# Down projection: gated tiles 3 to 18 as four block groups of four in one chain

## The chip, the cores and the metric

One core of one Trainium2 chip runs the whole program once. The metric is the device time of that launch in microseconds; the time before is the median of three runs.

## The reference, cut to what matters

Two layers of a sequence model, 1040 frames (16 meta tokens and 1024) by 1024 features, end each with a gated convolution block and a residual. The change lies in the last product of that block:

```python
def conv_ffn(x, w_up, conv_w, conv_b, w_down):
    h = x @ w_up
    ...
    u, g = jnp.split(hc, 2, axis=-1)
    return (jax.nn.silu(g) * u) @ w_down
...
h = h + conv_ffn(rms_norm(h, ffn_norm[i]), w_up[i], conv_w[i], conv_b[i], w_down[i])
```

silu(g) * u is 2816 wide, that is 22 tiles of 128 features, here called gated tiles; w_down turns them into 1024 output features, 8 output rows of 128.

## The kernel before

All data lie transposed: features on the 128 partitions, frames along the free axis, in two halves of 520 frames (layer 1, which drops the meta tokens at the end: 512). Every fp32 operand is split into a rounded part hi and a rest lo, and a product of two such operands is three matmuls (`mm3`, lines 256 to 258: hi x hi, lo x hi, hi x lo). A half of 520 frames is two pieces of 260 columns, a half of 512 one piece.

The up projection makes the gated tiles one by one and POOL's queue writes each to DRAM (`actd`). The residual stream lies in DRAM too (`hm`). The down projection (`ffn_down`, line 1648) then works through the tiles by a list, GROUPS. "n" is a plain group: for each of the 8 output rows and both halves it multiplies every tile, ACT copies the sum out of PSUM (line 1688), and an accumulating DMA of POOL's queue adds it to hm (line 1690). "r" is a plain group that adds on DVE straight to the residual, held in h tiles that were loaded from hm (`load_residual`, line 1658; line 1686). "s" is a block group (`down_blocks`, line 1557): the tiles, the output rows and the frames are each taken in two halves, and Strassen's scheme in Winograd's form computes the 2 x 2 x 2 block product with seven products instead of eight. The output rows go in four pairs j; a product is called (j, p) with p from 1 to 7. A group of eight tiles has four tiles to a product, a group of four has two.

For a product of a pair, `block_operand` (line 1109) makes the weight block: the raw blocks A11, A12, A21, A22 are loaded by SP, DVE combines them (line 1118: S1, S2, the difference for p = 7 in A21, S4), ACT casts hi (line 1136) and DVE subtracts to lo (line 1137). This is asked for AHEAD = 4 products early; hi and lo tiles alternate between two pools with three buffers each. After a product, `evacuate` (line 1593) empties PSUM: ACT copies after p = 1, 6, 7 and 4 (line 1596), DVE adds after p = 2, 5 or 7, and 3 (line 1595). Products 1, 6, 7 and 4 of a pair go on in the same bank, so PE may write p = 7 only after the copy of p = 6, and p = 4 only after that of p = 7; 5 and 3 share bank p2, which the add of p = 3 frees for the next pair's p = 5. A finished row is handed on (line 1584): accumulated into hm by POOL's queue (line 1590), or added on DVE to h (line 1587) where the residual is loaded already.

The block operands X1 to X7 of the moving side are made by a generator, `prepare` (line 1449): it loads four half-tile pairs by SP, forms four sums or differences on DVE (line 1519) and splits each of seven operands (ACT line 372, DVE line 373), eleven DVE rows and seven ACT casts of 1040 elements for four tiles. `pump` (line 1550) moves it on while slots (one-row SBUF buffers, 33 and 6) are free, and `complete` runs it until a group's operands are all there.

GROUPS before: tiles 0 to 2 plain, 3 to 10 a block group of eight, 11 to 14 plain onto the residual, 15 to 18 a block group of four; then `down_last` does 19 to 21. PE's order is the program's. The other engines' order is made by a scheduler, except for what `keep_in_program_order` pins.

## Time and profile before

| | us |
|---|---|
| median of 3 runs | 2485.22 (2484.97 to 2487.58) |
| the profiled execution | 2487.36 |
| its span | 2485.5 |
| PE busy | 2451.5 |
| DVE busy | 1879.0 |
| ACT busy | 1331.7 |
| down projection, layer 0: plain tiles begin, block group of four ends | 1006 and 1208 |
| down projection, layer 1: the same | 2240 and 2438 |

The span is the time between the program's first and last instruction; the profiled execution's own time is 1.9 us longer. Busy times are of one engine each, and the engines work side by side: only the one that the others wait for sets the time. A row of the timeline has the start, the duration, the engine, the line, the operation and the tiles (written<-read), and in brackets how long the engine stood idle before it and what ended that.

### The profile page before, as it was taken

To read this page: it belongs to the slowest core of one execution; us is meant where nothing else is said; L and a number is where in the kernel's file an instruction comes from. 1 tells how busy PE (TensorE), PEld (TensorE's weight loads), DVE (VectorE), ACT (ScalarE), POOL (GpSimd) and SP (SyncE) were. 2 spreads that over 40 slices of the span, in tenths; PEclk is the share of its full clock that TensorE was granted. 3 is DMA by queue.
4 is the path that set the end of the run, shared out by engine and by line. 5 is a ranking of instruction groups with operands and counts; after the bars stand their busy time and mean duration, and the time that the engine had idled before them with its cause. 6 is when DMAs were issued, how large, how long until landed. Compare 5 with 4: busy or idle time off the path is not lost.

```text
span 2485.5 us, 47396 instructions
## 1 busy us (share of the span) xinstructions
PE 2451.5 (99%) x18286; PEld 2358.8 (95%) x18286; DVE 1879.0 (76%) x3821; ACT 1331.7 (54%) x2889; POOL 388.3 (16%) x567
## 2 busy tenths in 40 slices
PE   9999999999999999999999999999999999999998
PEld 8989999999999999999999899999999999997887
DVE  7656776869988888865866666777799888887667
ACT  7346666636555555642543466665465555555433
POOL 2023333210000000100210334331100000001002
PEclk9999999999999999999999999999999999999999
DMA  4232134433322214764412222243423212247722
GB/s 134 69 88 70 45 97 128 127 124 102 119 76 80 90 66 143 196 165 126 129 43 70 75 79 72 67 147 106 147 84 110 90 64 90 83 159 168 213 72 87
DMA packets 122002, 261.02 MB, mean 105 GB/s; under 512 B 15264, under 2 KB 37024, under 8 KB 121776
## 3 DMA queue, kind: packets, MB, share of 16 engines
q1 hardware_dynamic: 97440, 182.81, 24.0%
q0 software_dynamic: 22464, 72.88, 10.4%
q8 instruction: 143, 2.34, 0.4%
q10 hardware_dynamic: 1872, 2.31, 0.3%
q14 instruction: 83, 0.68, 0.1%
HBM read 177.31 MB, written 67.85 MB: 99 GB/s over the span
## 4 chain that ended last, share of the span: by engine, by line
PE 70%; issue 15%; DVE 9%; ACT 4%; DMA 1%; POOL 1%; SPq 0%; DVEq 0%; POOLq 0%; ACTq 0%
PE mm L256 7%; PE mm L258 7%; PE mm L257 7%; PE up L257 6%; PE up L258 6%; PE up L256 6%; PE down L257 5%; PE down L256 5%; PE down L258 5%; PE av L755 3%; PE tr L729 2%; DVE S L696 1%; PE S L693 1%; PE wo L258 1%; PE wo L256 1%
## 5 line engine op out<-in xcount | busy, mean ns | idle before, releaser
L257 PE MATMUL up<-x,lo 128*128 128x260 f32 x2240 | 632.8, 283 | 1.1 <-DVE lo L1137 1.1
L256 PE MATMUL up<-x,hi 128*128 128x260 f32 x2240 | 632.9, 283 | 0.3 <-ACT hi L1136 0.3
L258 PE MATMUL up<-x,hi 128*128 128x260 f32 x2240 | 632.9, 283 | 0.0
L257 PEld LDWEIGHTS up<-x,lo 128*128 128x128 f32 x2240 | 421.7, 188 | 1.6 <-DVE lo L1137 1.5
L256 PEld LDWEIGHTS up<-x,hi 128*128 128x128 f32 x2240 | 421.6, 188 | 0.6 <-ACT hi L1136 0.5
L258 PEld LDWEIGHTS up<-x,hi 128*128 128x128 f32 x2240 | 421.9, 188 | 0.0
L1136 ACT CAST hi<-raw 128x512 fp32r<-128x512 f32 (+1 forms) x490 | 266.5, 553 | 210.8 <-PE up L258 91.3
L256 PE MATMUL mm<-xh,hi 128*128 128x348 f32 (+4 forms) x1056 | 362.9, 344 | 0.0
L1137 DVE TENSOR_TENSOR lo<-raw,hi 128x512 fp32r<-128x512 f32 (+1 forms) x490 | 287.6, 602 | 79.2 <-ACT hi L1136 78.7
L258 PE MATMUL mm<-xl,hi 128*128 128x348 f32 (+4 forms) x1056 | 339.9, 322 | 0.0
L257 PE MATMUL mm<-xh,lo 128*128 128x348 f32 (+4 forms) x1056 | 339.5, 321 | 0.0
L256 PEld LDWEIGHTS mm<-xh,hi 128*128 128x128 f32 x1056 | 199.5, 189 | 5.2 <-issue 4.6
L257 PEld LDWEIGHTS mm<-xh,lo 128*128 128x128 f32 x1056 | 199.5, 189 | 0.7 <-issue 0.7
L258 PEld LDWEIGHTS mm<-xl,hi 128*128 128x128 f32 x1056 | 198.4, 188 | 0.4 <-issue 0.3
L1118 DVE TENSOR_TENSOR raw<-raw,raw 128x512 f32<-128x512 f32 (+1 forms) x230 | 147.4, 650 | 32.0 <-DMA raw<-in_wd_dram 29.3
L708 ACT ACTIVATE P<-S,m 116x460 f32<-116x460 f32 (+2 forms) x224 | 125.0, 562 | 72.3 <-DVE m L696 68.6
L257 PE MATMUL down<-x,lo 128*128 128x260 f32 (+1 forms) x504 | 161.2, 320 | 0.4 <-DVE lo L1137 0.4
L256 PE MATMUL down<-x,hi 128*128 128x260 f32 (+1 forms) x504 | 161.1, 320 | 0.2 <-DVE dg L1595 0.2
L258 PE MATMUL down<-x,hi 128*128 128x260 f32 (+1 forms) x504 | 161.1, 320 | 0.0
L373 DVE TENSOR_TENSOR PT<-tr,PT 116x464 fp32r<-116x464 f32 (+3 forms) x240 | 123.0, 515 | 47.4 <-ACT PT L372 45.8
L223 ACT CAST hi<-raw 128x512 fp32r<-128x512 f32 (+2 forms) x152 | 87.3, 575 | 105.4 <-PE wo L258 34.0
L1397 POOL DMA_DIRECT2D actd<-cv x44 | 23.6, 537 | 737.4 <-DVE cv L1396 719.2
(308 smaller groups left out, 5985.6 us busy)
## 6 DMA issues: line engine op xcount, KB each, us to landing
raw<-in_wm_dram SPq DMA_DIRECT2D x330, 256.0 KB, 3.0
raw<-in_wd_dram SPq DMA_DIRECT2D x48, 256.0 KB, 4.6
actd<-cv POOLq DMA_DIRECT2D x22, 520.0 KB, 3.0
actd<-cv POOLq DMA_DIRECT2D x22, 512.0 KB, 3.2
cb<-cd SPq DMA_DIRECT2D x16, 520.0 KB, 4.0
hm<-h POOLq DMA_DIRECT2D x32, 260.0 KB, 3.1
kA<-kA SPq DMA_DIRECT2D x24, 260.0 KB, 4.1
kL<-kL SPq DMA_DIRECT2D x24, 260.0 KB, 4.7
```

Of the source, the lines that this page charges most:

```text
L223: nc.scalar.copy(hi[:, :n, :], raw[:, :n, :])
L256: nc.tensor.matmul(ps, wh, xh[:, c0:c0 + n], start=first, stop=False, skip_group_check=more)
L257: nc.tensor.matmul(ps, wl, xh[:, c0:c0 + n], start=False, stop=False, skip_group_check=more)
L258: nc.tensor.matmul(ps, wh, xl[:, c0:c0 + n], start=False, stop=last, skip_group_check=more)
L373: nc.vector.tensor_tensor(out=lo, in0=src, in1=hi.bitcast(F32), op=ALU.subtract)
L693: nc.tensor.matmul(S[:rows, :n], q["qA"][e][:, qs], q["kA"][e][:, c0:k1], start=True, stop=False)
L708: nc.scalar.activation(P[:rows, :n], S[:rows, :n], AF.Exp, scale=-1.0, bias=m[:rows, nch - 1:nch], accum_out=(den if nch == 1 else d3[:row ...
L729: nc.tensor.transpose(tr[:w, 3 - j, :rows], P[:rows, o:o + w], id_)
L755: nc.tensor.matmul(av[:, a:b], w.rearrange("p a b -> p (a b)"), x, start=(t == ts[0] and part == 0 and i == 0), stop=(t == last and i == 1))
L1118: nc.vector.tensor_tensor(out=q[out][:, :nk, :], in0=q[a][:, :nk, :], in1=q[b][:, :nk, :], op=op)
L1136: nc.scalar.copy(hi[:, :nk, :], src[:, :nk, :])
L1137: nc.vector.tensor_tensor(out=lo[:, :nk, :], in0=src[:, :nk, :], in1=hi[:, :nk, :].bitcast(F32), op=ALU.subtract)
```

## The change

Tiles 3 to 18 become four block groups of four, run as one chain of 16 row pairs: the sequence of products goes on across the group's borders, so the first product of a group stands among the last of the one before. The plain group "r" is gone. Rows of the first three groups, and the first pair of the fourth, are accumulated into hm by POOL's queue (24 and 2 of them, with LANDING = 8 products until a slot is free again); the residual's h rows are loaded in three portions at p = 6 of the fourth group's first three pairs, and its last three pairs are added to h on DVE. In a group of four, A11 and A12 come in one load into one tile, as do A21 and A22; S1 and S2 share a tile; the loads are asked for when the pair two before it reaches p = 6. Operands of the next group are pumped within the chain, two products out of three, and inside the chain the weight combines, weight splits and operand rows are pinned to program order (`placed`), while evacuations are not.

```diff
-GROUPS, LAST = (("n", 0, 3), ("s", 3, 8), ("r", 11, 4), ("s", 15, 4)), (19, 3)
+GROUPS, LAST = (("n", 0, 3), ("s", 3, 4), ("s", 7, 4), ("s", 11, 4), ("s", 15, 4)), (19, 3)
-LANDING = 4
+LANDING = 8
...
+            if nk == 2:
+                for names, src, own in ((("A11", "A12"), u, True), (("A21", "A22"), g, False)):
+                    t = self.wp.tile([128, 4, 128], F32, tag="raw", name="raw", bufs=4) if own else \
+                        fw.tile([128, 4, 128], F32, tag="raw2", name="raw2")
+                    nc.sync.dma_start(t[:], src)
...
+            self.placed(nc.vector.tensor_tensor(out=q[out][:, :nk, :], in0=q[a][:, :nk, :], in1=q[b][:, :nk, :], op=op))
...
+    def placed(self, ins):
+        if self.among_blocks:
+            self.tc.keep_in_program_order(ins)
...
+        self.placed(nc.scalar.copy(hi[:, :nk, :], src[:, :nk, :]))
+        self.placed(nc.vector.tensor_tensor(out=lo[:, :nk, :], in0=src[:, :nk, :], in1=hi[:, :nk, :].bitcast(F32),
+                                            op=ALU.subtract))
...
-            while len(ahead) < 2 and loads:
+            while len(ahead) < (1 if kind == "s" and self.among_blocks else 2) and loads:
...
+                    hi_ = nc.scalar.copy(h, src[:, :m, :W])
+                    lo_ = nc.vector.tensor_tensor(out=l, in0=src[:, :m, :W], in1=h.bitcast(F32), op=ALU.subtract)
+                    if self.among_blocks:
+                        self.tc.keep_in_program_order(hi_)
+                        self.tc.keep_in_program_order(lo_)
...
-                if nk == 2 and p == 6 and j + 1 < NP:
-                    self.block_raws(wd(2 * j + 2), wd(2 * j + 3), nk, j + 1, fw, raws)
+                if p == 6:
+                    for i in range(j + 1, min(j + 3, N)):
+                        self.block_raws(*wd(i), nk, i, fw, raws)
...
-            if hT:
+            m = 2 * (j % NP) + half
+            if j > N - NP:
...
+                if p == 1 and j % NP == 0:
+                    complete(lambda: built(groups[j // NP]))
...
+                if p == 6 and j >= N - NP and j < N - 1:
+                    load_residual({0: (2, 3), 1: (4, 5), 2: (6, 7, 0, 1)}[j - N + NP])
+                if i % 3 and (j >= N - NP or not built(groups[j // NP + 1])):
                     self.pump(1, 4)
```

`prepare` also got six more points at which it may pause among the blocks.

The first place is the beginning of layer 0's block groups on DVE, from the add onto dg of pair 0 to the first splits of pair 1. Line 1595 of before is 1628 of the change, 1118 is 1129, 1137 is 1152, 373 is 1532 and 1519 is 1539; raw2 names are S1, S2 or A21, st and t2 the operands' sums, du and dg the output rows. Before, in the group of eight:

```order
L1118 TENSOR_TENSOR raw2_14120<-raw2_13992,raw2_13994 128x512
L1118 TENSOR_TENSOR raw2_13992<-raw_13990,raw2_13992 128x512
L1137 TENSOR_TENSOR lo_13836<-raw_13630,hi_13835 128x512
L1137 TENSOR_TENSOR lo_13865<-raw_13642,hi_13864 128x512
L1118 TENSOR_TENSOR raw_13642<-raw_13642,raw2_13897 128x512
L1137 TENSOR_TENSOR lo_13900<-raw2_13897,hi_13899 128x512
L1118 TENSOR_TENSOR raw2_14122<-raw2_14120,raw_13990 128x512
L1595 TENSOR_TENSOR dg_13892<-down_13839,dg_13892 128x520
L1137 TENSOR_TENSOR lo_13930<-raw2_13895,hi_13929 128x512
L1595 TENSOR_TENSOR du_13772<-down_13903,du_13772 128x520
L1137 TENSOR_TENSOR lo_13961<-raw2_13638,hi_13960 128x512
```

Now, in the first group of four, with tiles 7 to 10's operands in it:

```order
L1628 TENSOR_TENSOR dg_13812<-down_13783,dg_13812 128x520
L1152 TENSOR_TENSOR lo_13780<-raw_13601,hi_13779 128x256
L1152 TENSOR_TENSOR lo_13797<-raw_13609,hi_13796 128x256
L1539 TENSOR_TENSOR st_13131<-st_13137,st_13131 128x1040
L1628 TENSOR_TENSOR du_13732<-down_13829,du_13732 128x520
L1539 TENSOR_TENSOR t2_13816<-st_13131,st_13128 128x1040
L1129 TENSOR_TENSOR raw2_13818<-raw2_13611 128x256
L1628 TENSOR_TENSOR du_13732<-down_13783,du_13732 128x520
L1129 TENSOR_TENSOR raw2_13818<-raw2_13818,raw_13609 128x256
L1539 TENSOR_TENSOR st_13128<-st_13137,t2_13816 128x1040
L1152 TENSOR_TENSOR lo_13822<-raw2_13818,hi_13821 128x256
L1532 TENSOR_TENSOR x6_13844<-t2_13816,x6_13843 128x1040
```

The split of (1,6), lo_13822, now follows two sums and a difference of the operands (st_13131, t2_13816, st_13128) and the two combines of its own pair; before, the combines stood early and no row of 1040 elements was there.

ACT at the same place, from the copy of (1,1) or the casts beside it. Before:

```order
L1596 COPY du_13803<-down_13778 128x520
L1136 CAST hi_13835<-raw_13630 128x512
L1596 COPY du_13772<-down_13747 128x520
L1136 CAST hi_13864<-raw_13642 128x512
L1136 CAST hi_13899<-raw2_13897 128x512
L1596 COPY dg_13892<-down_13747 128x520
L1136 CAST hi_13929<-raw2_13895 128x512
L1136 CAST hi_13960<-raw2_13638 128x512
L1596 COPY dg_13892<-down_13747 128x520
L1136 CAST hi_13998<-raw_13990 128x512
```

Now (line 1531 is the operand's cast, 1629 the copy out of PSUM, 1151 the weight's cast):

```order
L1629 COPY du_13751<-down_13738 128x520
L1531 CAST x1_13753<-st_13128 128x1040
L1151 CAST hi_13757<-raw2_13603 128x256
L1629 COPY du_13732<-down_13719 128x520
L1531 CAST x2_13774<-st_13134 128x1040
L1629 COPY dg_13812<-down_13719 128x520
L1151 CAST hi_13779<-raw_13601 128x256
L1151 CAST hi_13796<-raw_13609 128x256
L1629 COPY dg_13812<-down_13719 128x520
L1151 CAST hi_13821<-raw2_13818 128x256
L1531 CAST x6_13843<-t2_13816 128x1040
```

The casts x1, x2 and x6 of 1040 elements now stand between the copies of pair 0 and 1.

The second place is on DVE late in the chain. Before, in layer 0's group of four, from the combine S2 of pair 2 (raw2_15429), whose split lo_15432 stands three rows below the last of these:

```order
L1118 TENSOR_TENSOR raw2_15429<-raw2_15427,raw_15290 128x256
L1595 TENSOR_TENSOR dg_15279<-down_15250,dg_15279 128x520
L1137 TENSOR_TENSOR lo_15313<-raw2_15282,hi_15312 128x256
L1595 TENSOR_TENSOR du_15207<-down_15298,du_15207 128x520
L1137 TENSOR_TENSOR lo_15332<-raw2_15063,hi_15331 128x256
L1587 TENSOR_TENSOR h1_14678<-dg_15279,h1_14678 128x1040
L1595 TENSOR_TENSOR du_15207<-down_15250,du_15207 128x520
L1137 TENSOR_TENSOR lo_15350<-raw_15290,hi_15349 128x256
L1587 TENSOR_TENSOR h0_14676<-du_15207,h0_14676 128x1040
L1595 TENSOR_TENSOR du_15226<-down_15353,du_15226 128x520
L1137 TENSOR_TENSOR lo_15368<-raw2_15065,hi_15367 128x256
L1137 TENSOR_TENSOR lo_15386<-raw_15067,hi_15385 128x256
```

Now, in pairs 10 and 11 of the chain, with the operands of tiles 15 to 18:

```order
L1628 TENSOR_TENSOR dg_15256<-down_15226,dg_15256 128x520
L1152 TENSOR_TENSOR lo_15223<-raw_14824,hi_15222 128x256
L1539 TENSOR_TENSOR st_14921<-st_14921,t2_15071 128x1040
L1152 TENSOR_TENSOR lo_15241<-raw_14971,hi_15240 128x256
L1628 TENSOR_TENSOR du_15138<-down_15226,du_15138 128x520
L1532 TENSOR_TENSOR x4_15260<-st_14921,x4_15259 128x1040
L1129 TENSOR_TENSOR raw2_15263<-raw2_14973 128x256
L1628 TENSOR_TENSOR du_15287<-down_15334,du_15287 128x520
L1129 TENSOR_TENSOR raw2_15263<-raw2_15263,raw_14971 128x256
L1152 TENSOR_TENSOR lo_15267<-raw2_15263,hi_15266 128x256
```

The split of (11,6), lo_15267, stands right behind its combine (raw2_15263), and both behind the difference st_14921 and the split x4_15260 of the operands.

More of the change, by code (lines that the diff above doesn't have):

```diff
@@ L1655, in ffn_down, with load_residual @@
         two = lambda ap: ap.rearrange("p (a b) -> p a b", b=n)
-        hT, ahead, going = [], [], []
-        def load_residual():
-            for k in range(KD):
-                hT.append(s.get(F32, f"h{k}", first=ids))
-                nc.sync.dma_start(hT[k][:, o0:T], self.hm[k][:, o0:T])
+        hT, ahead, going = [None] * KD, [], []
+        def load_residual(which):
+            for k in which:
+                hT[k] = s.get(F32, f"h{k}", first=ids)
+                self.tc.keep_in_program_order(nc.sync.dma_start(hT[k][:, o0:T], self.hm[k][:, o0:T]))
         def complete(done):
@@ L1672, in plain @@
                 complete(lambda: all(j in acts for j in range(g0, g0 + ng)))
-                if kind == "r" and not hT:
-                    load_residual()
             if kind == "n" and m == 0:
@@ L1695, in plain @@
                     s.put(*acts.pop(j))
-            if not (nxt and built(nxt)):
+            if not (nxt and built(nxt[0])):
                 self.pump(2)
```

68 lines of the change are left out of this document (37 added, 31 removed).

## The prediction

> **What bounds the kernel now.** I read the engines' shares first, then the slices, then the down-projection stage by windows, and there who waits for whom.
>
> ```profile
> span 2485.5 us, 47396 instructions
> PE 2451.5 (99%) x18286; PEld 2358.8 (95%) x18286; DVE 1879.0 (76%) x3821; ACT 1331.7 (54%) x2889; POOL 388.3 (16%) x567
> PE   9999999999999999999999999999999999999998
> DVE  7656776869988888865866666777799888887667
> ```
>
> PE is busy in every slice, so time falls only where PE has less to do and nothing new holds it up. The stage is at 1006 to 1210 us in layer 0 and 2240 to 2438 us in layer 1. In the windows, PE's busy time is the third number after the clock-time pair, DVE's and ACT's follow.
>
> ```profile
> 1006.00:1041.00 35.00, 35.00 (x294) 35.00 (x293) 33.52 (x37) 27.31 (x41) 6.58 (x8) 1.00 0.79 175
> 1041.00:1120.00 79.00, 79.00 (x661) 79.00 (x660) 45.91 (x63) 33.89 (x53) 6.13 (x8) 1.00 0.71 183
> 1120.00:1165.00 45.00, 45.00 (x379) 45.00 (x378) 21.39 (x37) 7.01 (x13) 1.53 (x2) 1.00 0.47 148
> 1165.00:1210.00 45.00, 45.00 (x372) 45.00 (x371) 34.93 (x62) 23.33 (x50) 0.00 (x0) 1.00 0.18 50
> 2260.00:2300.00 40.00, 37.58 (x160) 29.61 (x159) 28.05 (x38) 21.15 (x36) 5.31 (x7) 1.00 0.78 173
> 2300.00:2365.00 65.00, 65.00 (x282) 52.70 (x281) 38.53 (x49) 27.04 (x40) 5.79 (x7) 1.00 0.80 217
> ```
>
> The first four rows are plain tiles 0 to 2, the block group of eight, plain tiles 11 to 14 and the block group of four of layer 0. PE never waits there, and DVE has 102.2 us of work in the 169 us of the last three. In layer 1 PE waits for little:
>
> ```profile
> PE down L256 <- ACT do L1688: 1.9, 1, 1.9
> PE down L257 <- DVE lo L1137: 0.4, 1, 0.4
> PE down L256 <- DVE dg L1595: 0.2, 1, 0.2
> ```
>
> **What it removes.** Plain tiles 11 to 14 take 8 rows x 2 halves x 4 tiles x 2 pieces x 3 = 384 matmuls in layer 0; as a block group, 4 pairs x 7 products x 12 = 336. Splitting the group of eight in two changes no count. So 48 matmuls of 260 columns go in layer 0, and 24 of 512 in layer 1, where a half is one piece. The windows price them: 79.00/661 = 0.1195 us and 65.00/282 = 0.2305 us. That is 5.7 + 5.5 = **11.3 us less on PE**, which has no cover, so all of it is on the path.
>
> **What it adds.** Each product now has two tiles where the group of eight had four: 12 matmuls, 1.43 us (1.38 us in layer 1) instead of 2.87. The block operands of groups two to four (eleven DVE rows of 1040 elements and seven ACT casts each) are made inside the chain. Before, the ones of the last group were made under the plain tiles. DVE prices:
>
> ```profile
> 1110.35 1.24 DVE L1498 TENSOR_TENSOR al<-st,ah 128x1040 fp32r<-128x1040 f32 x1
> 1111.51 1.23 DVE L373 TENSOR_TENSOR x<-st,x 128x1040 fp32r<-128x1040 f32 x1
> 1112.66 1.24 DVE L1519 TENSOR_TENSOR t<-st 128x1040 f32<-128x1040 f32 x1
> 1113.81 0.69 DVE L1595 TENSOR_TENSOR du<-down,du 128x520 f32<-128x520 f32 x1
> ...
> 1185.74 0.69 DVE L1595 TENSOR_TENSOR dg<-down,dg 128x520 f32<-128x520 f32 x1
> 1186.35 0.41 DVE L1137 TENSOR_TENSOR lo<-raw,hi 128x256 fp32r<-128x256 f32 x1
> 1186.68 0.41 DVE L1118 TENSOR_TENSOR raw<-raw,raw 128x256 f32<-128x256 f32 x1
> ```
>
> Start to start a row of 1040 costs 1.155 us, of 520 0.61, of 256 0.335; whoever waits for it sees it after the whole 1.24, 0.69 or 0.42. A pair has 7 lo rows, 4 combines and 3 adds: 11 x 0.335 + 3 x 0.61 = 5.5 us, in 10.0 us of PE. Over 16 pairs, with 33 operand rows, 3 splits of late tiles and 6 adds to h, that is 88 + 42 x 1.155 = 137 us in 160. On average it fits; pair by pair it doesn't: the sums of the order's rows between two dg adds are 11.9 us in pair 1 and 10.6 and 11.3 in pairs 5 and 6.
>
> The Trainium skill (VectorE: DVE Perf Modes, "The DRAIN you can't avoid") says that the next operation starts only when the pipe is empty. By that rule a row would cost its whole duration, the same rows would come to some 161 us, and the stalls below to some 7 us more a layer, 2509 us in all. Here the trace disagrees (1.155 us from start to start at 1.24 us long), and the rows decide.
>
> ACT and DVE take their rows in the order that the section on the change shows, and operand casts are now kept between weight splits and evacuations. ACT's prices:
>
> ```profile
> 1167.51 0.28 PE L256 MATMUL down<-x,hi 128*128 128x260 f32 x1
> ...
> 1169.14 0.59 ACT L1596 COPY du<-down 128x520 f32<-128x520 f32 x1 [1.03 <-PE down L258]
> 1169.63 0.41 ACT L1136 CAST hi<-raw 128x256 fp32r<-128x256 f32 x1
> ...
> 1180.66 0.41 ACT L1136 CAST hi<-raw 128x256 fp32r<-128x256 f32 x1 [1.06 <-PE down L258]
> 1180.98 1.06 ACT L1497 CAST ah<-st 128x1040 fp32r<-128x1040 f32 x1
> ...
> 1195.78 1.06 ACT L1497 CAST ah<-st 128x1040 fp32r<-128x1040 f32 x1
> 1196.74 0.59 ACT L1596 COPY dg<-down 128x520 f32<-128x520 f32 x1
> ```
>
> A cast takes 0.96, a copy 0.49, a weight cast 0.32 us to the next row; an evacuation begins some 0.2 us after PE's last issue (the group of four began at 1167.51, so its first product was issued by 1168.94, and its copy began at 1169.14). With these I added the rows of the order by hand, counting from the chain's start.
>
> **Pair 1**: the copy of (1,1) begins at 2 x 1.43 + 0.2 = 3.07; the cast x1 is behind it and ends at 4.62; DVE is idle until then. Up to the lo row of product (1,6) DVE has five rows of 1040 (5.78), three adds (1.82), three combines (1.0), three lo rows (1.0) and that row's own 0.42, and waits 0.4 for the cast x2: 4.66 + 10.4 = 15.1. PE wants it as the second matmul of the tenth product, at 9 x 1.434 + 0.12 = 13.0. **Stall 2.0 us**; what is queued behind is all of PE.
>
> **Pairs 5 and 6**, likewise: the lo rows of (5,7), (6,1) and (6,2) are 0.6, 0.6 and 0.8 late, each behind an operand row, and the add that frees bank p2 for (6,5) is 1.2 late behind x5, x7 and a difference: 3.3 us with small change. **Pairs 9 to 11**: copy (9,6), behind cast x2, holds (9,7) for 0.65; lo (9,3), behind x6, is 1.8 late; lo (11,1) 0.7; lo (11,6), behind x4, whose cast waits for a DVE difference, 3.1: 6.3 us. Together **11.6 us in layer 0**. Layer 1 has nearly the same rows, its pair of PE work is 9.7 us instead of 10.0 and its DVE rows 1.5% shorter: I take 12.
>
> Bounds: if DVE never waited for ACT, its rows alone are still late: 1.6 in pair 1; 17.6 us of rows from 0.8 against the 17.2 at which (6,5) starts, 1.3; 21.7 us from 6.3 against 27.3 at (11,6), 0.7. So 3.6 us a layer is the low end, unless the order's lead hides even that, and 0 the lowest. The nearest row of its kind, the last group of layer 1, has 0.6 us of stalls with 8 adds to h and 3 splits (11 rows of 1040) in it, so it is not empty; but there a pair's combines stand up to 14 rows ahead of the splits that use them, and now next to them. I take the row-by-row value, and keep both ends.
>
> **Other edits.** A row pair's weights come as two loads of 256 KB, asked for two pairs (20 us) ahead; accumulations into hm become 26 a layer instead of 8.
>
> ```profile
> raw<-in_wd_dram SPq DMA_DIRECT2D x20, 256.0 KB, 5.1
> hm<-do POOLq DMA_DIRECT2D x8, 520.0 KB, 8.2
> raw<-in_wd_dram SPq DMA_DIRECT2D x16, 128.0 KB, 2.1
> ...
> 1048.34 0.59 ACT L1596 COPY du<-down 128x520 f32<-128x520 f32 x1 [3.15 <-DMA hm<-do]
> ```
>
> A load of 5.1 us is hidden by 20 us of lead. An accumulation of 8.2 us frees its slot after 8 products, 11.4 us; 24 of them in 120 us are a rate of 0.20 a us against 0.23 in the plain stage (8 in 35 us, DMA 0.79 busy), so they fit, at nothing; if not, ACT's copy waits for its slot, as for 3.15 us in the last row. The residual loads stand on SP behind accumulations that end 13 us or more earlier, and only the last tiles' weights are behind them. One wait goes: in layer 1 ACT stood 2.92 us at a weight cast with the copies of the plain tiles behind it,
>
> ```profile
> 2268.81 1.66 ACT L1136 CAST hi<-raw 128x512 fp32r<-128x512 f32 x3 [2.92 <-DMA raw<-in_wd_dram]
> 2271.00 0.50 PE L256 MATMUL down<-ah,hi 128*128 128x512 f32 x1 [1.87 <-ACT do L1688]
> ```
>
> and PE lost 1.87 us. Now the first such cast stands two rows of output earlier and fewer operand casts compete with the copies, so I count 1.9 gained (bounds 0 and 1.9).
>
> **Sum.** -11.3 - 1.9 + 11.6 + 12 = +10.4 us. The profiled execution took 2487.4 us (its span 2485.5 and 1.9 around it), 2.2 above the median of 2485.2: 2497.8 on it, **2495 us** on the median.
>
> **Rivals.** *The stalls are mostly absorbed*: for it, PE stands 0.6 us in all of the old groups of four; against it, the sums of 11.9 and 11.3 us in a 10 us pair. With 3.6 a layer: 2485.2 - 13.2 + 7.2 = 2479, with none 2472. It decides for the change below 6.6 us of stall a layer. Chance 0.20. *Half of the stalls* (7 a layer, if casts start earlier than I reckon): 2486, chance 0.22. *Late accumulations*: DMA was 0.71 to 0.80 busy; for it, that copy at 1048; against it, the rate above. Three such waits beside the stalls: 2505, chance 0.10. *The clock falls*: the trace keeps a granted clock of 1.00 through the 1.87 us wait; a gap of 3.1 us at (11,6) is longer than any it shows here. If the clock halved for 3.4 us after one such gap a layer, that would be 3.4 us more, 2499 us, inside the range; chance 0.05. The Trainium skill (TensorE: Matmul & The Clock Gate, "What's actually happening") has PE at half clock after an idle window of about 3.4 us. Whether a gap here reaches that, no trace of before shows.
>
> The forecast keeps 0.43. The range goes from 2477, which leaves out the lower part of the first rival, to 2505. A measurement here tells 0.2%, 5 us, from no change: faster 0.20, within it 0.22, slower 0.58.
>
> **What would show it.** PE should have 72 matmuls less; waits of PE for lo rows (L1152) and copies in the down stage of 8 us or more a layer, in pairs 1, 5, 6 and 9 to 11; DVE above 85% in the chain; the 1.9 us for do gone. If PE's waits there sum to under 6.6 us a layer, the prediction's sign is wrong; if they stand on DMA, its cause.

## The result, and the profile after

The changed kernel takes **2508.47 us** (median of 4 runs, 2504.62 to 2509.34) against 2485.20 in the same session: a ratio of **1.0088, 95% interval 1.0071 to 1.0106**, 23.3 us slower. The direction is the one forecast; 2495 us and the range's end of 2505 us are both too low. The profiled execution of after is its fastest, 2504.62 us (a span of 2502.8), so the traces differ by 2504.62 - 2487.36 = 17.3 us; the other 6.0 lie in where the two profiled executions stand in their spread (3.9 below the median after, 2.2 above it before).

The head of the page after, with the line of the accumulations' queue (packets, MB, share):

```profile
span 2502.8 us, 47711 instructions
PE 2451.3 (98%) x18214; PEld 2351.0 (94%) x18214; DVE 1930.2 (77%) x4007; ACT 1386.0 (55%) x3055; POOL 418.5 (17%) x603
PE   9999999999999999999999999999999999999998
DVE  7656777769988888687866666777799888885887
q0 software_dynamic: 27648, 91.90, 14.8%
```

The 72 matmuls are gone (18286 to 18214), and PE's busy time is nevertheless the same: a matmul that follows a wait counts as busy for longer, and so does one at a lower clock. The slices show nothing of the loss, since no wait is over 3 us. It is found by asking for PE's waits in the down projection of layer 0 (1000 to 1260 us: in total, times, longest),

```profile
PE down L256 <- ACT hi L1151: 5.0, 4, 2.6
PE down L257 <- DVE lo L1152: 2.9, 5, 0.9
...
PE down L256 <- ACT do L1722: 0.6, 1, 0.6
PE down L256 <- ACT du L1629: 0.5, 1, 0.5
```

where before had none, and in layer 1 (2240 to 2503):

```profile
PE down L256 <- ACT hi L1151: 5.9, 5, 2.7
PE down L257 <- DVE lo L1152: 2.5, 5, 0.8
PE down L256 <- ACT do L1722: 2.2, 1, 2.2
PE down L256 <- DVE du L1628: 1.1, 1, 1.1
...
PE down L256 <- ACT du L1629: 0.6, 1, 0.6
```

The times of layer 0's waits, from the timeline of PE (start, length, and in brackets how long PE stood and for what):

```profile
1056.04 0.39 PE L256 MATMUL down<-x,hi 128*128 128x260 f32 x1 [1.00 <-ACT hi L1151]
1057.03 0.39 PE L257 MATMUL down<-x,lo 128*128 128x260 f32 x1 [0.61 <-DVE lo L1152]
1103.35 0.39 PE L257 MATMUL down<-x,lo 128*128 128x260 f32 x1 [0.40 <-DVE lo L1152]
1108.66 0.39 PE L257 MATMUL down<-x,lo 128*128 128x260 f32 x1 [0.57 <-DVE lo L1152]
1112.67 0.36 PE L256 MATMUL down<-x,hi 128*128 128x260 f32 x1 [0.97 <-ACT hi L1151]
1145.05 0.39 PE L256 MATMUL down<-x,hi 128*128 128x260 f32 x1 [0.51 <-ACT du L1629]
1150.14 0.39 PE L256 MATMUL down<-x,hi 128*128 128x260 f32 x1 [0.51 <-ACT hi L1151]
1151.45 0.39 PE L257 MATMUL down<-x,lo 128*128 128x260 f32 x1 [0.92 <-DVE lo L1152]
1159.48 0.39 PE L257 MATMUL down<-x,lo 128*128 128x260 f32 x1 [0.42 <-DVE lo L1152]
1168.14 0.57 PE L256 MATMUL down<-x,hi 128*128 128x260 f32 x1 [2.56 <-ACT hi L1151]
```

Counting the matmuls from the chain's start, these are products (1,6), (6,1), (6,2), (6,5), (9,7), (9,3), (11,1) and (11,6): the places that the prediction had named, but for (5,7), which is in time. The waits in brackets understate the loss, because the pipe has to fill again. What a place costs is better read from the matmuls done in a stretch (the count behind PE's busy time; DVE and ACT are the third and fourth pair, then POOL, the granted clock, the DMA share):

```profile
1040.00:1060.00 20.00, 18.39 (x150) 17.90 (x149) 14.66 (x25) 10.93 (x22) 2.54 (x3) 1.00 0.82 156
...
1100.00:1120.00 20.00, 17.92 (x139) 16.81 (x139) 18.56 (x34) 13.24 (x26) 2.15 (x3) 1.00 0.92 211
...
1140.00:1160.00 20.00, 17.65 (x139) 16.73 (x139) 17.09 (x27) 10.82 (x21) 3.11 (x4) 1.00 0.69 134
1160.00:1180.00 20.00, 17.44 (x130) 17.00 (x130) 15.24 (x31) 10.06 (x22) 2.56 (x3) 0.91 0.88 244
...
2280.00:2300.00 20.00, 18.35 (x75) 14.13 (x74) 14.20 (x24) 10.77 (x21) 3.38 (x4) 0.95 0.86 164
2300.00:2320.00 20.00, 20.00 (x85) 16.21 (x84) 15.32 (x34) 11.99 (x27) 3.40 (x4) 0.96 0.60 116
...
2340.00:2360.00 20.00, 16.51 (x65) 11.45 (x63) 17.41 (x29) 12.03 (x24) 1.70 (x2) 1.00 0.82 181
...
2380.00:2400.00 20.00, 17.81 (x73) 13.11 (x72) 16.89 (x28) 11.33 (x22) 3.40 (x4) 1.00 0.71 145
2400.00:2420.00 20.00, 17.18 (x71) 12.96 (x72) 16.95 (x34) 10.70 (x24) 3.43 (x4) 1.00 0.91 251
```

An undisturbed stretch of 20 us holds 169 matmuls in layer 0 and 88 in layer 1 (the kernel without operand rows, below). So pair 1 costs (169 - 150) x 0.118 = 2.2 us, pairs 5 and 6 3.5, pairs 9 to 11 8.2: **14.0 us in layer 0**. In layer 1 it is 3.6, 5.2 and 7.3: **16.1 us**. The granted clock is under 1.00 in three of these rows; before, it was 1.00 through the whole stage.

Another measure, used for every kernel below, is the length of the down projection, from the start of its first matmul to that of its last, from the timeline. Before it is 201.3 us in layer 0 and 197.9 in layer 1, after 211.0 and 207.7. That is +19.5 us. The work between the two stages was 2.0 us shorter in this one execution (1029.7 against 1031.6), which the change does not touch; those of the runs below have 1028.7 to 1032.7 there.

### The profile page after: what moved, and what is told of

It reads as the page before. It is cut to its first block, busy times and chain, and to the rows that moved or that the text cites. A ratio compares the mean times of both kernels' runs of the same rounds, so it can differ in the third digit from the quotient of the medians.

```text
span 2502.8 us, 47711 instructions
## 1 busy us (share of the span) xinstructions
PE 2451.3 (98%) x18214; PEld 2351.0 (94%) x18214; DVE 1930.2 (77%) x4007; ACT 1386.0 (55%) x3055; POOL 418.5 (17%) x603
## 4 chain that ended last, share of the span: by engine, by line
PE 80%; DVE 11%; ACT 5%; issue 2%; DMA 2%; POOL 0%; SPq 0%; DVEq 0%; ACTq 0%; POOLq 0%
PE up L257 10%; PE up L256 10%; PE up L258 10%; PE mm L256 7%; PE mm L258 7%; PE mm L257 7%; PE down L257 4%; PE down L256 4%; PE down L258 4%; PE av L755 3%; PE tr L729 2%; DVE S L696 1%; PE S L693 1%; PE wo L258 1%; PE wo L257 1%
## 5 line engine op out<-in xcount | busy, mean ns | idle before, releaser
L1152 DVE TENSOR_TENSOR lo<-raw,hi 128x256 fp32r<-128x256 f32 (+1 forms) x602 | 315.2, 543 | 109.8 <-ACT hi L1151 109.0
L1151 ACT CAST hi<-raw 128x256 fp32r<-128x256 f32 (+1 forms) x602 | 292.3, 505 | 184.2 <-PE up L258 89.7
L256 PE MATMUL down<-x,hi 128*128 128x260 f32 (+1 forms) x672 | 217.4, 323 | 13.2 <-ACT hi L1151 10.9
L257 PE MATMUL down<-x,lo 128*128 128x260 f32 (+1 forms) x672 | 219.0, 326 | 5.5 <-DVE lo L1152 5.4
L258 PE MATMUL down<-x,hi 128*128 128x260 f32 (+1 forms) x672 | 216.1, 322 | 0.0
L1129 DVE TENSOR_TENSOR raw<-raw,raw 128x512 f32<-128x512 f32 (+1 forms) x262 | 153.1, 588 | 15.1 <-DMA raw<-in_wd_dram 12.3
L256 PEld LDWEIGHTS down<-x,hi 128*128 128x128 f32 x672 | 127.5, 190 | 27.8 <-ACT hi L1151 14.5
L257 PEld LDWEIGHTS down<-x,lo 128*128 128x128 f32 x672 | 127.4, 190 | 20.8 <-DVE lo L1152 11.3
```

Source lines behind the costliest of these rows:

```text
L256: nc.tensor.matmul(ps, wh, xh[:, c0:c0 + n], start=first, stop=False, skip_group_check=more)
L257: nc.tensor.matmul(ps, wl, xh[:, c0:c0 + n], start=False, stop=False, skip_group_check=more)
L258: nc.tensor.matmul(ps, wh, xl[:, c0:c0 + n], start=False, stop=last, skip_group_check=more)
L1129: self.placed(nc.vector.tensor_tensor(out=q[out][:, :nk, :], in0=q[a][:, :nk, :], in1=q[b][:, :nk, :], op=op))
L1151: self.placed(nc.scalar.copy(hi[:, :nk, :], src[:, :nk, :]))
L1152: self.placed(nc.vector.tensor_tensor(out=lo[:, :nk, :], in0=src[:, :nk, :], in1=hi[:, :nk, :].bitcast(F32), op=ALU.subtract))
```

## The experiments

Three theories were set against each other. **A**, the prediction's: operand rows of 1040 elements stand bunched on DVE among the weight splits, in a kept order, and single pairs ask for more than 10 us. **B**: transfers (26 accumulations, larger weight loads) are late. **C**: the kept order itself is the harm. Later a fourth question came up, the clock. Line numbers of experiments differ from after's by up to nine. Ratios are to the kernel before, run beside each on the same chip.

| kernel | median, us | ratio, 95% interval | down stage, layers 0 and 1, us |
|---|---|---|---|
| before | 2485.2 | 1 | 201.3, 197.9 |
| after | 2508.5 | 1.0088 (1.0071 to 1.0106) | 211.0, 207.7 |
| e_noprep | 2478.7 | 0.9975 (0.9964 to 0.9985) | 196.4, 189.9 |
| e_nolo | 2488.8 | 1.0011 (1.0002 to 1.0021) | 201.4, 196.2 |
| e_nopin | 2549.5 | 1.0261 (1.0246 to 1.0276) | 232.3, 230.3 |
| e_lopool | 2552.8 | 1.0271 (1.0256 to 1.0287) | 235.9, 231.3 |
| e_lead3 | 2522.1 | 1.0154 (1.0140 to 1.0168) | 218.6, 218.4 |
| e_ahead5 | 2499.4 | 1.0055 (1.0038 to 1.0071) | 203.6, 204.4 |
| e_lead8 | 2497.2 | 1.0052 (1.0039 to 1.0064) | 206.6, 203.8 |
| e_lead8raw | 2498.8 | 1.0058 (1.0044 to 1.0071) | 208.1, 204.8 |
| e_early | 2520.1 | 1.0141 (1.0127 to 1.0155) | 216.1, 218.3 |
| e_spread | 2496.7 | 1.0047 (1.0034 to 1.0059) | 204.1, 205.5 |
| e_spread8 | 2482.5 | 0.9991 (0.9982 to 0.9999) | 197.8, 198.1 |
| e_s8pin | 2479.5 | 0.9978 (0.9969 to 0.9987) | 197.4, 194.7 |
| e_fill | 2513.7 | 1.0114 (1.0100 to 1.0128) | 213.4, 213.8 |
| e_gap | 2594.4 | 1.0440 (1.0424 to 1.0456) | 255.7, 249.4 |
| e_fill11 | 2505.3 | 1.0080 (1.0066 to 1.0094) | 209.4, 209.8 |
| e_fill11b | 2505.3 | 1.0080 (1.0067 to 1.0094) | 210.3, 210.8 |
| e_after2 | 2507.6 | 1.0084 (1.0070 to 1.0098) | 210.7, 212.9 |

### Is it the operand rows?

**e_noprep**: operands of the second to fourth group are neither loaded nor made, and the products use the first group's.

```
+            if g0 != 3:
+                continue
...
-                    _, hi, lo = X[g0][p][k // 2]
+                    _, hi, lo = X[3][p][k // 2]
```

> Leaves out the making of the block operands of the second, third and fourth group (their loads, casts, lo rows and differences; their products use the first group's operands), so the output is not the reference's. Weights, splits of weights, products, evacuations and accumulations stay. If the operand rows inside the chain are what delays PE (theory A), the waits of PE in the chain go, the granted clock stays at 1.00 there, and the 72 matmuls less show in full: 2474 to 2479 us. If the 26 accumulations or the weight loads are the cause (theory B), the waits at the same places stay and the time is above 2495. If the operands are only half of it, 2485 to 2492.

Measured 2478.65 us. All accumulations and weight loads are still there, and no product of the chain waits in either layer; the row in which after did 130 matmuls at a clock of 0.91 is full again:

```profile
1160.00:1180.00 20.00, 20.00 (x169) 20.00 (x168) 15.16 (x31) 12.06 (x25) 3.41 (x4) 1.00 0.91 204
```

The DMA share is 0.91, as high as in after (0.88). B is out, as far as accumulations and weight loads go; the loads of the operands, which this run lacks too, are kept in the next one. It is also about the most that the change could bring: 5.8 us under before by the medians. In the traces the two stages are 12.8 us shorter, as 11.3 for the matmuls and the waits that are gone would have it, and the rest of the program 2.7 longer. This trace has three falls of the clock outside the two stages (0.91 at 0 to 20, 440 to 460 and 1680 to 1700 us, 1.8 us each), which the profile of before has not; they would account for the 2.7 and more. The rest of the difference between 12.8 and 5.8 is where the two profiled executions stand in their spread (2.9 above the median of before beside it, 1.4 below its own); why before's stands so high stays open.

**e_nolo**: a part of that, only the lo rows of those operands left out, and with them the buffers that the rows were written to.

```
-                    lo = get(f"x{p}", F32R) if m == 2 else hi
+                    lo = hi if self.among_blocks else get(f"x{p}", F32R)
```

> Leaves out the lo rows of the operands that are made in the chain (the third pass of each product reads the hi part in their place), so the output is not the reference's. Casts, differences, loads, weights, products and evacuations stay. If it is the amount of DVE work beside the weight splits that makes PE wait (theory A), taking 21 of 33 operand rows a layer, 24 us of 137, away leaves under 2 us of waits a layer: 2478 to 2486 us, 65 to 75 us below the kernel that has the same rows on POOL. If it is the loads, the casts on ACT or the slots, the waits stay: 2495 to 2508.

Measured 2488.79, just outside what A said. The 24 us of DVE rows bring back 20 of the 23 us. What is left in the chain are waits of 0.3 to 0.9 us, most for copies that stand behind operand casts on ACT (in layer 0: du 1.5 us in 2 waits, dg 0.6, lo 0.6, hi 0.3). So DVE's rows are the main part, and ACT's casts a small one; the loads of the operands are all there and are not it. That the free buffers had no part in it is not shown.

### Is it the order?

**e_nopin**: the casts, lo rows and differences of the block groups are free to be placed.

```
     def placed(self, ins):
-        if self.among_blocks:
-            self.tc.keep_in_program_order(ins)
+        pass
```

> All of the work stays; the casts, lo rows and differences of the block groups are no longer kept in program order, so the scheduler places them as it did before the change. If the kept order is the cause (theory C), most of the stalls go: 2480 to 2490 us. If the amount of operand work per pair is the cause whatever its order (theory A), stalls of 10 us or more a layer stay, at other places: 2500 to 2515.

Measured 2549.53: C is wrong by its sign. The kept order saves 41 us; without it PE stands up to 7.8 us at a time for evacuations.

**e_lopool**: the lo rows of the operands go to POOL.

```
-                    lo_ = nc.vector.tensor_tensor(out=l, ...
+                    lo_ = (nc.gpsimd if self.among_blocks else nc.vector).tensor_tensor(out=l, ...
```

> The seven lo rows of each operand group that is made in the chain go from DVE to POOL (a row of 512 takes 1.30 us there, so 1040 some 2.6, and 7 rows a group are 18 us in 40). Theory A: DVE has 21 x 1.155 = 24 us less to do a layer in the chain, nearly all stalls go, 2478 to 2486 us. Rival: POOL and DVE rows of two SBUF inputs hold each other up (the Trainium skill, SBUF - State Buffer, section SBUF: two separate sides), then a DVE row beside a POOL row takes up to 2.6 us longer and as much is lost as is won: 2500 to 2515.

Measured 2552.76, worse than both theories' figures. POOL's row, and the DVE row that begins beside it:

```profile
1059.48 2.69 POOL L1532 TENSOR_TENSOR x<-t,x 128x1040 fp32r<-128x1040 f32 x1
```

```profile
1059.63 2.83 DVE L1152 TENSOR_TENSOR lo<-raw,hi 128x256 fp32r<-128x256 f32 x1
1062.38 0.41 DVE L1129 TENSOR_TENSOR raw<-raw,raw 128x256 f32<-128x256 f32 x1
```

A weight split of 0.42 us takes 2.83, and ends 0.29 us behind the POOL row. An add, which has one of its two inputs in PSUM, is not held up; it keeps its 0.69 us beside a POOL row of 1091.72 to 1094.36, and the combine behind it is stretched to the row's end:

```profile
1091.95 0.69 DVE L1628 TENSOR_TENSOR dg<-down,dg 128x520 f32<-128x520 f32 x1
1092.56 2.09 DVE L1129 TENSOR_TENSOR raw<-raw 128x256 f32<-128x256 f32 x1
```

So POOL is no help here: each of its rows takes DVE's splits, combines and operand rows away for its whole length. The Trainium skill (SBUF — State Buffer, "SBUF: two separate sides") calls the port pair that DVE and GpSimd share an exclusive lock, held for a whole instruction, where DVE has two SBUF inputs; these rows agree.

### Is it the bunching, or too little lead?

**e_lead3**, **e_ahead5**, **e_lead8**: weight splits three, five or eight products ahead. The constant of e_ahead5 also rules the up projection, which was not meant; its down stage is what counts here.

```
-AHEAD = 4
+AHEAD = 5
```

> Weight operands are made five products ahead instead of four, with the same six pairs of tiles. If PE waits because its weight splits stand too late in the order (theory A, by 0.6 to 3.1 us a place), one product more of lead, 1.4 us, takes the small stalls away (pairs 5 and 6, copies) and shortens the long ones of pairs 1 and 11 by up to 1.4 each: 2490 to 2498 us. If the sixth tile comes free too late, since it waits for the product that has just been issued, nothing is won: 2503 to 2512.

For three and eight the chain has a constant of its own; for eight, hi and lo share one tile:

```
-                ensure(i + AHEAD)
+                ensure(i + DOWN_AHEAD)
...
+            t = pool.tile([128, 4, 128], F32R, tag=tag, name="hl", bufs=3)
+            hi, lo = t[:, 0:2, :], t[:, 2:4, :]
```

> Weight splits in the chain three products ahead instead of four. Theory A: each of some five late places a layer is later by up to one product, 1.4 us, and new ones appear: 2516 to 2528 us. Rival (evacuations are what is late): 2506 to 2512.

> All of the work and its order of operand rows stay, but each product's weight splits in the chain are made eight products ahead instead of four (hi and lo of a product packed into one tile, of which each was half empty). If PE waits because single pairs ask DVE for more than 10 us while the average fits (theory A), four products or 5.7 us more of lead cover the 11.9 us of pair 1 and the 11.3 of pair 6, nearly all waits go, and the time is near the one without operand rows, 2476 to 2484 us. If it is the evacuations that wait behind operand casts and differences on ACT and DVE (rival), the lead does not help them: 2492 to 2500, with waits for copies and adds left.

Measured 2522.1, (2508.5 with four), 2499.4 and 2497.2. From three to five a product of lead is worth 9 to 14 us, about as A says (five came out 1.4 us above its range). Eight brings hardly more, so A's figure fails there. Its waits are of another kind:

```profile
1185.32 0.59 PE L257 MATMUL down<-x,hl 128*128 128x260 f32 x1 [3.38 <-DVE du L1636]
```

In layer 0 no product waits for a weight split any more; 7.1 us of waits for adds onto du and dg remain, in the same queue of DVE. A was half of it, its rival the other half. Whether the adds are late from the splits made so early or from the operand rows, e_spread8 tells.

**e_spread**: the makers of operands are stepped after every second product.

```
-                if i % 3 and (j >= N - NP or not built(groups[j // NP + 1])):
+                if i % 2 and (j >= N - NP or not built(groups[j // NP + 1])):
```

> All of the work stays; the makers of operands are stepped after every second product instead of two of three, so that the rows of 1040 elements per pair are 4, 2, 2, 1, 4, 3, 4, 0, 2, 5, 3, 1, ... instead of 5, 1, 2, 2, 5, 5, 0, 0, 4, 4, 3, 1. If the bunching of operand rows in pairs 1, 5, 6 and 9 to 11 is what makes DVE late (theory A), the waits of pairs 1 and 5 to 6 go or halve, and those of pairs 10 and 11 stay: 2497 to 2503. If the bunching is not the cause, 2506 to 2511.

**e_spread8**: this and the lead of eight together.

> The wider spacing of operand rows together with the lead of eight products for weight splits. The lead of eight left no wait for weight splits but waits of 0.7 to 3.4 us for the adds of evacuations, which stood behind operand rows in pairs 1, 6 and 11; with fewer rows together there these shrink. Theory A: 2484 to 2491 us. If the adds are late from the weight splits made so early and not from operand rows, 2494 to 2499 as with the lead alone.

Measured 2496.67 and 2482.47, both a little under A's ranges: one character takes 12 us away without an instruction less, and with the lead it is 26 us. Each alone leaves the other's waits: the spacing those for weight splits, the lead those for adds. With both, layer 0's chain has no wait, although the splits are made as early as with the lead alone; so the adds were late from the operand rows. This settles A with that addition: with the same rows, only spaced and asked for earlier, the stages are 1.4 and 8.2 us longer than without them (of the 8.2, 2.2 are the wait for do, below, 3.1 two waits for adds and 1.8 a fall of the clock behind the wait for do), instead of 14.6 and 17.8.

**e_early**: operands of the second group are begun among the plain tiles.

```
-            if not (nxt and built(nxt[0])):
+            if not (nxt and built(nxt[1])):
```

> The plain tiles go on making operands after the first group's are built, as far as tiles for them are free, so that DVE has less to do in the first pairs of the chain. Theory A: the waits of pair 1 (1.6 to 1.7 us recorded a layer, some 2.2 of PE's time) go, the later ones stay or shift, 2500 to 2506 us. If no tiles are free that early, nothing changes: 2505 to 2511.

Measured 2520.11, 12 us slower where A said 2 to 8 faster. The operand rows did leave pairs 1 and 2 (5 and 1 in after's order, none here), but the operands share their buffers with the plain tiles' outputs, and the cast of an operand now waits until an accumulation has landed and frees one:

```profile
1047.65 1.06 ACT L1531 CAST x<-st 128x1040 fp32r<-128x1040 f32 x1 [3.11 <-DMA hm<-do]
```

PE then stands 3.71 us for the weight cast behind this one. Room, not DVE, is short there.

### The wait for a plain tile's copy

The prediction had counted 1.9 us for it as going. In after it is 2.17 us, and the rows of SP's queue and ACT say why:

```profile
2259.53 2.59 SPq L1104 DMA_DIRECT2D raw<-in_wd_dram  x2
```

```profile
2271.07 0.40 ACT L1151 CAST hi<-raw 128x256 fp32r<-128x256 f32 x1 [8.50 <-DMA raw<-in_wd_dram]
```

The chain's first weight load takes 11.5 us from its issue to the cast (such loads take 4.5 in the median) beside a DMA share of 1.03 to 1.06 at 2260 to 2270 us, and ACT's copies stand behind that cast.

**e_lead8raw** should ask for the load one plain tile earlier.

```
+                    if nxt and k == len(part) - 3:
+                        blocks[2]()
```

> As with the lead of eight, and the first pair's two weight loads are asked for one plain tile (4.4 us) earlier. If the wait of PE for the copy of a plain tile (0.6 us in layer 0, 2.2 in layer 1) comes from ACT standing at the first weight cast for its load, these go as well: 2 to 3 us less than with the lead alone, 2474 to 2481. If the load is not the cause, the same time as with the lead alone.

Measured 2498.76, no gain (1.7 us of wait left). It tested nothing: the load was still issued 12.1 us after the stage's start, against 12.4 in after, since its place in SP's queue is not the code's.

**e_s8pin**: in e_spread8, the plain tiles' copies and the first weight casts are kept in order, the casts behind the copies. (The earlier request of e_lead8raw is in it too, again without effect: the first load is issued 12.2 us after the stage's start, as in e_spread8.)

```
-                        blocks[0](2 * (k - len(part) + 2) + 1)
-                    plain(*t, ahead[k], nxt)
+                    plain(*t, ahead[k], nxt)
+                    if nxt and k >= len(part) - 2:
+                        self.among_blocks = True
+                        blocks[0](2 * (k - len(part) + 2) + 1)
...
-                    nc.scalar.copy(x, ps[:, :pieces, :n])
+                    self.tc.keep_in_program_order(nc.scalar.copy(x, ps[:, :pieces, :n]))
```

> Wider spacing and lead of eight, and the copies of the plain tiles and the first weight casts of the chain are kept in program order, the casts behind the copies of the last two tiles. The wait of PE for the copy of a plain tile (2.2 us in layer 1, with a clock fall of 1.7 behind it) came from ACT standing 8.5 us at the first weight cast, whose load took 11.7 us beside a DMA share of over 1.0. If the cast's place is the cause, that wait and fall go: 2476 to 2480 us, under the kernel before by 5 to 9. If PE then waits for the first products' weight splits instead, 2481 to 2486.

Measured **2479.51**, the version that beats both kernels: 0.9978 of before (0.9969 to 0.9987), 1.2% under after. Layer 0's stage has no wait of PE at all; layer 1's (2236 to 2432) has

```profile
PE down L257 <- DVE du L1636: 3.5, 2, 2.5
PE down L257 <- ACT du L1637: 0.2, 1, 0.2
```

and the wait for do is gone. Its median is within a microsecond of the kernel that makes no operands, though in the traces its stages are 1.0 and 4.8 us longer.

### The clock

In after the granted clock is 0.91 at 1160 to 1180 us. Matmul by matmul, behind the wait of 2.56 us:

```profile
1168.98 0.42 PE L258 MATMUL down<-x,hi 128*128 128x260 f32 x1
1169.19 0.42 PE L256 MATMUL down<-x,hi 128*128 128x260 f32 x1
...
1171.83 0.28 PE L257 MATMUL down<-x,lo 128*128 128x260 f32 x1
1171.95 0.28 PE L258 MATMUL down<-x,hi 128*128 128x260 f32 x1
```

From 1168.98 to 1171.36 eleven matmuls are 0.216 us apart, then 0.12 again. With the first two, which take 0.84 us instead of 0.24, a fall costs 11 x 0.096 + 0.6, some 1.6 us (1.8 by the granted clock of the window, 0.09 x 20).

**e_fill** puts unused matmuls ahead of three products to keep PE at work.

```
+FILL = {(1, 6): 4, (6, 6): 3, (11, 6): 9}
...
+                    for _ in range(FILL[j, p] * pieces):
+                        nc.tensor.matmul(x[:, 0, :n], lhsT=last[0], rhs=last[1], start=True, stop=True)
```

> All of the work stays, and PE gets extra matmuls whose results nobody uses (they go to a bank that is begun anew right after), ahead of the products (1,6), (6,6) and (11,6) of each chain: 8, 6 and 18 of 260 columns in layer 0, 4, 3 and 9 of 512 in layer 1, that is 1.0, 0.7 and 2.1 us, a little less than PE stands there. If the granted clock falls because PE stands idle for 1.2 to 2.7 us (theory: each fall costs the 1.7 us that the windows show, 0.90 and 0.93 of 10 us), the clock stays at 1.00 at those places and the kernel is faster for having more to do: 2500 to 2505, mean clock 0.997 or 0.998. If the falls have nothing to do with the idle time, 2508 to 2512 and the falls stay.

Measured 2513.74, a miss. The unused matmuls waited for their own bank, 2.5 us in layer 0, and the clock fell behind that wait instead. At (11,6), where the bank was free, it did not fall in either layer.

**e_gap**: known idle times, in the kernel without operand rows.

```
+ROWS = {2: 5, 4: 6, 6: 7, 8: 8, 10: 9, 12: 10}
...
+                if p == 6 and j in ROWS:
+                    for _ in range(ROWS[j]):
+                        self.placed(nc.vector.tensor_tensor(out=rows[0][:, 0:T], in0=rows[0][:, 0:T], in1=rows[0][:, 0:T], op=ALU.subtract))
```

> The kernel without the operands of groups two to four (output not the reference's, and no waits of its own in the chain), with idle rows of DVE put ahead of the lo row of product (j,6): 5, 6, 7, 8, 9 and 10 rows of 1040 elements in pairs 2, 4, 6, 8, 10 and 12 of each chain, of which the lead of four products hides some 5 us, so that PE stands for about 1, 2, 3, 4, 5 and 6.5 us. Theory on the clock: each time PE stands over some 1 to 3 us, 1.7 us of clock follow, and the time lost at a place is its idle time plus 1.7, 3.4 for the longest: idle of some 43 us and clock of 17 to 25, together 2538 to 2550 us. If the clock has nothing to do with idle time, the granted clock stays at 1.00 and the time is 2518 to 2526.

Measured 2594.37. The lead hid less than reckoned, so the waits are 4.1 to 10.6 us, 88.4 in all, outside the lengths that the question was about. Every one of the twelve is followed by a fall, of 3.1 to 6.2 us:

```profile
1224.58 0.59 PE L257 MATMUL down<-x,hi 128*128 128x260 f32 x1 [10.47 <-ACT hi L1152]
...
1229.54 0.42 PE L257 MATMUL down<-x,hi 128*128 128x260 f32 x1
...
1230.34 0.29 PE L259 MATMUL down<-x,hi 128*128 128x260 f32 x1
```

The matmuls are 0.42 long until 1229.5, 5 us after the wait, and 0.29 from then on. The kernel is 115.7 us over e_noprep; 88.4 are waits, and the other 27.3 are 2.3 us for each wait, clock and refilled pipe together.

**e_fill11** has the filling ahead of (11,6) alone, and ran twice, the second time (e_fill11b) beside the unchanged kernel (e_after2).

```
-FILL = {(1, 6): 4, (6, 6): 3, (11, 6): 9}
+FILL = {(11, 6): 9}
```

> All of the work stays; unused matmuls (2.1 us) stand only ahead of product (11,6), where PE waits 2.6 to 2.7 us and where the bank that they write is free, so that they bring no wait of their own, as those of pairs 1 and 6 did. If the fall of the clock at 1160 to 1180 us comes from PE standing idle there, no window of pairs 11 and 12 is under 1.00 and the time is 2 to 4 us under the changed kernel's: 2503 to 2507. If not, 2508 to 2511.

> The changed kernel as it is, beside the next one on the same chip. Theory on the clock: the places of PE's waits repeat to 0.1 us, and which of them are followed by a fall of the clock differs from run to run, so that times between 2504 and 2510 go with mean clocks between 0.997 and 0.994, about 1.6 us a fall.

> The longest wait, ahead of product (11,6), filled with unused matmuls, on the same chip as the unchanged one. If falls of the clock follow idle time of PE, this one has fewer of them, a mean clock higher by 0.001 to 0.002, and is 2 to 4 us faster. If not, both are within 1 us.

Measured 2505.25 and 2505.32, and 2507.62 for the unchanged kernel: with 2.1 us of work more a layer it is 2.3 us faster. The intervals of the ratios overlap, so the times alone don't settle it; the traces at the place itself speak for it. Behind (11,6) the clock does not fall in the two traces of e_fill11, nor in that of e_fill: none in six places. In the two of the unchanged kernel it fell there in layer 0 both times, in layer 1 once: three in four. Elsewhere the filled kernels have falls as before. The row of e_fill11 to set against after's x130 at 0.91:

```profile
1160.00:1180.00 20.00, 19.51 (x158) 18.95 (x157) 15.37 (x31) 10.65 (x24) 3.41 (x4) 1.00 0.97 259
```

The second trace of the unchanged kernel has each of layer 0's chain waits within 0.03 us of the first's, and up to 2460 us it has five falls in its windows, one of them twice as long as the others, where the first has three: 2508.91 us at a mean clock of 0.995 against 2504.62 at 0.997. By the windows that is 10.6 us of clock against 5.4; 4.3 us were measured between the two, with the wait for do 0.9 us longer in the second. So falls of the clock account for the difference between these two executions. One fall of each trace, at 1690 us, lies outside the down projection. Over all nine executions of this kernel time and clock go together only loosely: one of 2505.09 us has a mean clock of 0.995, one of 2507.62 has 0.997.

## Why the prediction came out as it did

**What it removes: right.** 72 matmuls less, and nothing took the place of their 11.3 us.

**Where PE waits: right.** Of the nine products that were named, eight wait in layer 0 and all nine in layer 1, with (5,3) besides. The row-by-row sum gave 2.0, 3.3 and 6.3 us for pairs 1, 5 to 6 and 9 to 11; measured were 2.2, 3.5 and 8.2, of which the last includes a fall of the clock, 0.09 x 20 = 1.8 us. Without it layer 0 is 12.2 against 11.6.

**Layer 1: mis-sized.** "I take 12" was carried over, not worked out. Measured: 16.1, less 1.8 of clock (0.05 x 20 + 0.04 x 20) is 14.3. Pairs 5 and 6 gave 5.2 instead of layer 0's 3.5. The trace shows one difference: adds are not pinned, and in layer 1 an add at 2336.98 us stands ahead of two weight splits of pair 5, with DVE idle for 0.54 us until PE is done, where in layer 0 the splits go first; (5,7), in time in layer 0, waits 0.99 us here. What that is worth was not tried. In both layers the price of some rows was a little low: a row that reads what the row ahead of it wrote starts later than I had it. In e_gap, whose added rows do so, each further row of 1040 elements lengthened PE's wait by 1.28 us (4.09, 5.37, 6.64), not 1.155.

**"so I count 1.9 gained": failed.** The wait for do stayed at 2.2 us. The first cast does stand earlier in the order, but its load was late, beside transfers that filled the DMA engines, and the order of ACT put the copies behind it. e_s8pin, with the casts behind the copies, has no such wait.

**The clock: the step that failed most.** "If the clock halved for 3.4 us after one such gap a layer, that would be 3.4 us more" was a rival at 0.05, with the argument that the trace kept 1.00 through a wait of 1.87 us. It is what happened, with that size, in the profiled execution (1.8 + 1.8), and more often in others. That the size agrees is in part luck: (11,6) stood 2.56 us, not 3.1, and in layer 1 the fall came behind the waits of 1.17 and 0.48 us in pair 1. One wait without a fall was taken as evidence for the next.

So, against +10.4: 2.9 of waits, 3.6 of clock and 1.9 for do make +18.8; the traces show +17.3, with 2.0 us less between the stages. From there to the median's +23.3 it is 2.2 for the profiled execution of before and 3.9 for that of after, which had three falls of the clock, at a mean of 0.997, where the other three had means of 0.994 and 0.995. The prediction's other sum, 2509 us with each DVE row at its whole duration, lies near the median by luck: rows of 1040 elements still start some 1.155 us ahead of the next row in after, and the time came from the terms above.

**Other edits at nothing: right.** The loads and accumulations cost no wait in the chain:

```profile
raw<-in_wd_dram SPq DMA_DIRECT2D x64, 256.0 KB, 4.5
...
hm<-du POOLq DMA_DIRECT2D x13, 520.0 KB, 6.4
```

The accumulations of 6.4 us are no slower than the 8.2 that the prediction reckoned with, and e_noprep keeps them all without a wait.

**DVE above 85%: wrong.** In the chain's windows above it is 14.2 to 18.6 of 20 us, up to 93%, but 134.9 us in 1041 to 1211, 79%: PE's waits stretch the stage, and a DVE in a kept order is late while it also stands idle (for hi casts above all). This is why the average said that it fits.

## What to carry to other kernels

Work moved beside a busy engine has to fit stretch by stretch, within the lead that its consumers have; the average over the stage says nothing, and spacing it or giving more lead (26 us here, from both) is cheaper than removing it. Lead alone moves the wait to the evacuations in the same queue. And where a tuned kernel has PE at full clock throughout, count each new wait of a microsecond or more with a chance of 1.6 us on top: in the two traces of the unchanged kernel, 6 of the 16 waits of 0.96 us or more in the down projection have a fall within 4 us behind them.

## What the runs showed of the hardware that was not expected

**The clock falls after waits far under 3.4 us, and not always.** With one fall: 1.17 and 0.48 us within 1.5 us (layer 1, pair 1), and 2.56. Without: 1.00 and 0.61 in both traces of the unchanged kernel (the same in e_fill11b had one), 1.87 in before, 2.45 in e_s8pin, 2.66 in layer 1 of after; the same 2.66 in the second trace had one. The Trainium skill (TensorE: Matmul & The Clock Gate, "What's actually happening") has PE at half clock after an idle window of some 3.4 us, a window that runs freely, so that the point of change depends on where in it an event lies. That the same wait differs from run to run agrees, and so, roughly, do the 3.1 to 6.2 us that a fall lasted in e_gap; that a wholly idle window is needed does not, since PE worked within any 3.4 us around all waits of after.

**A POOL row stops DVE rows with two inputs in SBUF**, not those with one in PSUM: a split of 0.42 us became 2.4 to 2.8 us, an add stayed at 0.69, and 42 POOL rows of some 2.5 us cost 44 us.

**DVE rows that depend on each other** are 1.28 us apart instead of 1.155 for 1040 elements (e_gap against before).
